# Block 2's first four units take the rows before layer norm, and the norm is applied to their results

## The chip, the cores and the metric

The kernel runs on one core of one Trainium2 chip. The metric is the device time of one execution in microseconds. TensorE (PE) does the matrix products and writes PSUM; VectorE (DVE), ScalarE (ACT) and GpSimd (POOL) do the elementwise work, and POOL has no access to PSUM; SyncE (SP) issues the DMAs. Each engine takes its instructions in the order in which they were written down for it, and waits for the other engines by semaphores.

## The reference

Three blocks run one after the other on a sequence of 512 positions with 2048 features, in float32. What matters here is the start of block 2, on the result of block 1:

```
def second_block(x, c, w_ada, b_ada, w_in, ...):
    mod = jax.nn.silu(c) @ w_ada[l] + b_ada[l]
    shift, scale, gate = jnp.split(mod[:, None, :], 3, axis=-1)
    h = _layernorm(x) * (1.0 + scale) + shift
    proj = h @ w_in[l]
    u, v, z_a, q, k, v_b, z_b = jnp.split(proj, IN_SPLITS, axis=-1)
    y_a = _spatial_gating(jax.nn.gelu(u), jax.nn.gelu(v), z_a, ...)
    ...
```

`x` there is the RMS-normed output of block 1. Layer norm needs mean and variance over all 2048 features of a position, so every one of them must be known before the first normed value is.

## The kernel before

Activations lie transposed: a tile has 128 features in its partitions and the 512 positions along the free dimension, so the 2048 features are 16 tiles (index `k`). A weight matrix is worked off in **units**: one unit makes 128 output features, as 16 steps of `k`. Float32 accuracy comes from splitting: weights and rows are each taken as `hi` (rounded to the matmul's format, on ACT) and `lo` (the rest, on DVE), and each step has three products 128x128 by 128x512 (`hi*hi`, `hi*lo`, `lo*hi`), so a unit has 48 of them. The weights' parts are called `wh` and `wl`; the chunks they come from, 4 steps of a unit each, are split on ACT and DVE while PE works.

Block 1 ends in its output projection, 16 units. `out1_tile` adds the input, centres it on a rough mean (`d`, kept in `ds`), and adds up the three sums that the norms need. `out1_end` handles the last tile: 24 sums over partitions on PE (`stat_sum`) in the last unit and 24 after it (`stat_last`), then seven operations on 128x4 columns and two powers on POOL give the factors `g` and `c` of the norm (`x*g + c`). PE spreads them over the partitions with 16 small products (`bcast_cols`). Meanwhile PE runs 27 products whose results nobody reads (`warm`). `make` then builds the normed row of step `k`: two DVE operations (times `g`, plus `c`, both read from PSUM), on ACT the scaling with `1 + scale` and `shift`, and the split into `hi` and `lo`.

`first_units` runs the first four units of block 2 (output tiles 8, 0, 16 and 9) side by side, step by step, as the rows become ready; the last four steps are done unit by unit. From the fifth unit on all 16 rows are there, and units run one after the other (`drive`), each request of a consumer (`sgu` for the spatial gating) in its turn. The results of the first four units stay in PSUM until `sgu` reads them.

The order on each engine is found by a scheduler at build time from the order of the program and its own durations; from `out1_end` up to the end of `first_units`' set-up it is held to the program's order for DVE, ACT and PE (`in_order`). Tiles come from pools with a fixed number of buffers for a tag: 7 for `e`, 9 for `w`, 20 for `y`, 5 each for `wh` and `wl`, 3 for raw weight chunks. A tile waits until its buffer is free.

Beside the units of blocks 1 and 2 a background queue (`bgq`, one step for each weight chunk) computes the modulations `mod2` and `mod3` (`mods`: 6 slices of 16 loads of 512 KB with one DVE operation 128x1024 each, and two steps on PE and DVE) and a bias table. `sc2` is `1 + scale` and `1 + gate` of block 2.

Of the kernel before, what the change touches and what calls it, by code (L numbers as in the profile page):

```python
# [34 lines left out]
FIRST2 = (8, 0, 16, 9)  # L35
# [5 lines left out]
class Kernel:  # L41
# [188 lines left out]
            except StopIteration as e:  # L230
                return e.value

    def first_units(self, w, cts, make, chunks, side=None, tail=None):

        rhs, pss, has = [], [], {}
        for _ in cts:
            self.n += 1
            pss.append(self.pm.tile([P, T], F32, name=f"pm{self.n}", tag="m"))  # L240

        def take(chunks):
            for u, k0, hl in chunks:
                has[u] = has.get(u, []) + [(k0, hl)]

        def product(k, u):
            k0, (hi, lo) = [c for c in has[u] if c[0] <= k][-1]
            c, ps = slice((k - k0) * P, (k - k0 + 1) * P), pss[u]
            self.mm(ps, hi[:, c], rhs[k][0], start=k == 0, stop=False)
# [415 lines left out]
    def mods(self, wada, c, b, mod):  # L665
# [6 lines left out]
        for sl in range(6):  # L672
# [10 lines left out]
            for half in range(2):  # L683
# [3 lines left out]
                self.tt(o, o, self.col(b, 8 * sl + 4 * half, 4), OP.add)  # L687
                yield


    def stat_begin(self, n):
        self.acc = [self.k(f"acc{i}") for i in range(n)]
# [36 lines left out]
    def out1(self, ys):  # L729
        ysp = [self.split(v) for v in ys]  # L730
        self.stat_begin(3)
        ds = []
        self.sc2 = self.cp.tile([P, 32], F32, name="sc2")
        for ct in range(KT - 1):
            self.out1_tile(ct, self.unit(self.A["wo1"], ct, ysp), ds)
        self.ts(self.sc2, self.mod2[:, 16:48], 1.0, None, OP.add)
        with self.in_order():
            args = self.out1_end(ysp, ds)
        return self.first_units(self.A["w2"], FIRST2, *args)

    def out1_tile(self, ct, ps, ds):
        nc = self.nc
# [17 lines left out]
        return (0, d), (2, sx), (1, sq)  # L760

    def out1_end(self, ysp, ds):
        nc = self.nc
        last, ps = self.last_unit(self.A["wo1"], ysp, self.stat_sum)
# [4 lines left out]
        m, v, a, g, c = (self.s(4) for _ in range(5))  # L769

        self.ts(a, ps[:, 8:12], LN_EPS / D, LN_EPS * EPS)
        self.ts(m, ps[:, 0:4], 1.0 / D)
        self.stt(v, ps[:, 4:8], 1.0 / D, a, OP.mult, OP.add)
        self.tt(c, m, m)
        self.tt(v, v, c, OP.subtract)
        nc.gpsimd.tensor_tensor(g, v, self.nhalf[:, :4], OP.pow)
        self.r1 = self.cp.tile([P, 4], F32, name="r1")
        self.ts(a, ps[:, 8:12], 1.0 / D, EPS)
        nc.gpsimd.tensor_tensor(self.r1, a, self.nhalf[:, :4], OP.pow)
        self.stt(c, m, -1.0, g, OP.mult, OP.mult)  # L780
        chunks = self.end(self.first_chunks(self.A["w2"], FIRST2, 0))
        gb, cb = self.bcast_cols(g), self.bcast_cols(c)
        self.warm(9, ysp[15][0])
        mod = self.mod2

        def make(k):
            t1 = self.t()
            self.tt(t1, ds[k], gb)
            self.tt(t1, t1, cb, OP.add)
            self.act(t1, t1, AF.Identity, scale=self.sc2[:, k:k + 1], bias=mod[:, k:k + 1])  # L790
            hi, lo = self.a(), self.a()
            self.act(hi, t1)
            yield
            yield
            self.tt(lo, t1, hi.bitcast(F32), OP.subtract)
            return hi, lo

        return make, chunks


    def sgu(self, g, h, w, ys):
# [879 lines left out]
def _wtile(w, perm=None):  # L1681

    K, N = w.shape
    return np.ascontiguousarray(
        w.reshape(K // 1024, 8, P, N // P, P).transpose(3, 0, 2, 1, 4).reshape(N // P, K // 1024, P, 1024))


def _rpb_rows(r):
# [92 lines left out]
```

## Time and profile before

| | us |
|---|---|
| median of 3 runs (lowest, highest) | 3410.37 (3408.67, 3417.95) |
| the profiled execution | 3414.3 |
| its span in the profile | 3412.6 |
| PE busy (mean granted clock 0.996) | 3370.2, 99% |
| PE weight loads | 2777.0, 81% |
| DVE busy | 2010.0, 59% |
| ACT busy | 1272.6, 37% |
| POOL busy | 131.5, 4% |
| DMA | 451.64 MB, 132 GB/s on average |

A row of the profile names a line of the kernel, an engine, an operation, and the tiles as output <- inputs without their numbers: `pm` are the sums of units in PSUM, `x` other PSUM tiles, `a` rows split for the matmul, `wr`, `wh`, `wl` raw weights and their two parts, `t` work tiles of the tags `w`, `e` and `y`, `s` small columns, `ga` and `gr` the background's sum and load. Times are in microseconds from the start of the span unless ns stands there. Matmuls are pipelined: one takes 0.39 us or so from start to end, and the next starts before.

### The profile page before, as it was taken

The numbers are of one execution on the slowest core, as the hardware profiler recorded it, in microseconds if no ns is written. First come the engines' busy times: TensorE is split into PE (matmuls) and PEld (weight loads), VectorE is DVE, ScalarE is ACT, GpSimd is POOL, SyncE is SP. The second block draws the span as 40 slices with busy tenths as digits, with TensorE's granted clock in tenths as the row PEclk, the third lists the DMA queues.
The fourth block names the chain that finished last, engine by engine and source line by source line (L and its number), as shares of the span: only waits on it lengthen the run. The fifth ranks groups of instructions, "written<-read, shape, count | busy, mean of one in ns | idle before, by whom it ended". The sixth has DMA issues, their size and how long they took to land.

```text
span 3412.6 us, 43830 instructions
## 1 busy us (share of the span) xinstructions
PE 3370.2 (99%) x16336; PEld 2777.0 (81%) x16336; DVE 2010.0 (59%) x3793; ACT 1272.6 (37%) x2459; POOL 131.5 (4%) x156
## 2 busy tenths in 40 slices
PE   9999999999999999999999999999999999999999
PEld 7877877877888888888888888887888888888887
DVE  8677566657777555643367667756755443344552
ACT  4222244444334223444442243333334444432331
POOL 0000000000000000101100000000000000000000
PEclk9999999999999999999999999999999999999999
DMA  6355345435663445532234333332222233324442
GB/s 223 124 179 173 132 153 185 152 120 191 211 218 128 161 156 175 170 119 96 84 105 146 99 107 109 96 98 84 85 72 87 96 108 104 128 99 143 141 146 92
DMA packets 166166, 451.64 MB, mean 132 GB/s; under 512 B 26496, under 2 KB 47296, under 8 KB 165952
## 3 DMA queue, kind: packets, MB, share of 16 engines
q1 hardware_dynamic: 165952, 448.84, 39.6%
q8 instruction: 128, 2.10, 0.3%
q14 instruction: 86, 0.70, 0.1%
HBM read 423.58 MB, written 25.18 MB: 132 GB/s over the span
## 4 chain that ended last, share of the span: by engine, by line
PE 86%; DVE 7%; DMA 3%; issue 2%; ACT 1%; POOL 0%; SPq 0%; DVEq 0%; ACTq 0%; POOLq 0%
PE pm L128 76%; PE x L128 8%; DMA gr<-in_wada_dram 3%; PE x L638 1%; DVE wl L117 1%; PE x L134 1%; DVE ga L120 1%; DVE t L117 1%; DVE fp L117 1%; DVE t L120 1%; DVE ft L1290 1%; ACT t L114 0%; ACT wh L114 0%; DMA t<-in_xt_dram 0%; DVE t L527 0%
## 5 line engine op out<-in xcount | busy, mean ns | idle before, releaser
L128 PE MATMUL pm<-a,wh 128*128 128x512 f32 x8512 | 2669.2, 394 | 6.2 <-ACT a L114 3.6
L128 PEld LDWEIGHTS pm<-a,wh 128*128 128x128 f32 x8512 | 1575.4, 189 | 335.9 <-issue 15.6
L128 PE MATMUL pm<-a,wl 128*128 128x512 f32 x4256 | 1665.5, 391 | 0.5 <-DVE wl L117 0.5
L114 ACT ACTIVATE wh<-wr 128x512 fp32r<-128x512 f32 (+2 forms) x1073 | 671.6, 627 | 1714.5 <-PE pm L128 1570.9
L117 DVE TENSOR_TENSOR wl<-wr,wh 128x512 fp32r<-128x512 f32 (+2 forms) x1073 | 738.1, 690 | 913.5 <-ACT wh L114 843.7
L128 PEld LDWEIGHTS pm<-a,wl 128*128 128x128 f32 x4256 | 801.3, 188 | 172.9 <-DVE wl L117 0.9
L120 DVE SCALAR_TENSOR_TENSOR ga<-gr,sc_c,ga 128x1024 f32<-128x1024 f32 x180 | 231.1, 1284 | 80.5 <-DMA gr<-in_wada_dram 79.7
L114 ACT ACTIVATE t<-t 128x512 f32<-128x512 f32 (+2 forms) x204 | 125.0, 613 | 147.7 <-DVE t L117 101.4
L114 ACT ACTIVATE t<-x 128x512 f32<-128x512 f32 (+4 forms) x301 | 143.7, 505 | 83.1 <-PE x L128 50.7
L117 DVE TENSOR_TENSOR t<-t,t 128x512 f32<-128x512 f32 (+2 forms) x233 | 155.8, 669 | 23.2 <-ACT t L114 19.0
L128 PE MATMUL x<-t,t 128*128 128x128 f32 (+8 forms) x1104 | 146.1, 295 | 7.5 <-DVE t L117 7.4
L128 PEld LDWEIGHTS x<-t,t 128*128 128x128 f32 (+3 forms) x1104 | 117.8, 175 | 33.7 <-issue 19.3
L114 ACT ACTIVATE t<-t,s 128x512 f32<-128x512 f32 (+2 forms) x192 | 98.5, 513 | 96.0 <-DVE s L527 63.0
L142 POOL TENSOR_TENSOR s<-s,nhalf 128x4 f32<-128x4 f32 (+1 forms) x51 | 61.2, 1201 | 1247.9 <-DVE s L125 1247.9
L638 PE MATMUL x<-cst,t 128*128 128x128 f32 x464 | 66.7, 275 | 5.8 <-DVE t L124 3.8
L120 DVE SCALAR_TENSOR_TENSOR t<-t,pm 128x512 f32<-128x512 f32 x64 | 43.7, 684 | 46.1 <-PE pm L128 46.0
L638 PEld LDWEIGHTS x<-cst,t 128*128 128x128 f32 x464 | 55.5, 144 | 17.1 <-DVE t L124 6.1
L114 ACT ACTIVATE t<-pm 128x512 f32<-128x512 f32 (+2 forms) x154 | 68.9, 482 | 0.2
L117 DVE TENSOR_TENSOR a<-t,a 128x512 fp32r<-128x512 f32 x96 | 63.7, 686 | 8.8 <-ACT a L114 8.7
L128 PE MATMUL x<-acc,t 128*128 128x256 f32 (+3 forms) x336 | 66.4, 297 | 0.0
L134 PE MATMUL x<-cst,t 128*128 128x128 f32 x400 | 60.3, 273 | 6.1 <-DVE t L117 2.9
L134 PEld LDWEIGHTS x<-cst,t 128*128 128x128 f32 x400 | 48.3, 140 | 19.8 <-DVE t L120 2.9
(232 smaller groups left out, 1663.9 us busy)
## 6 DMA issues: line engine op xcount, KB each, us to landing
wr<-in_w_dram SPq DMA_DIRECT2D x380, 512.0 KB, 3.3
gr<-in_wada_dram SPq DMA_DIRECT2D x192, 512.0 KB, 4.3
wr<-in_wo_dram SPq DMA_DIRECT2D x96, 512.0 KB, 3.4
t<-in_xt_dram SPq DMA_DIRECT2D x32, 256.0 KB, 4.0
res<-t SPq DMA_DIRECT2D x32, 256.0 KB, 2.1
t<-res SPq DMA_DIRECT2D x32, 256.0 KB, 2.7
gld<-t SPq DMA_DIRECT2D x32, 256.0 KB, 2.0
t<-gld SPq DMA_DIRECT2D x32, 256.0 KB, 2.8
```

Of the source, the lines that this page charges most:

```text
L114: return self.nc.scalar.activation(out, in_, fn, **kw)
L117: return self.nc.vector.tensor_tensor(out, a, b, op)
L120: return self.nc.vector.scalar_tensor_tensor(out, a, s, b, op0=op0, op1=op1)
L128: return self.nc.tensor.matmul(out, l, r, start=start, stop=stop, skip_group_check=True)
L134: self.nc.tensor.transpose(b[:, p * P:(p + 1) * P], src[:, p * P:(p + 1) * P], self.ident)
L142: self.nc.gpsimd.tensor_tensor(out, u, self.nhalf[:, :n], OP.pow)
L638: self.nc.tensor.transpose(b[:, j * P:(j + 1) * P], src, self.ident)
L1290: nc.vector.tensor_reduce(tv[:, :, i], pv, AX, OP.add, negate=True)
```

## The change

The first four units no longer wait for the norm. They multiply the weights with `ds[k]` times `1 + scale`, without `g` and `c`. Since the norm is the same for all features of a position, it can be applied to a unit's result: result times `g`, plus `c` times the sum of the scaled weights, plus the sum of the weights times `shift`. These two sums for each output feature (`uv2`) are computed in the background beside block 1 (`first_sums`, a new queue entry between `mods` of block 2 and of block 3, from a copy `w2f` of the four units' weights).

The 27 products of `warm` are gone, and so is the program's order by hand. The last sums are formed after step 1, the spreads after step 3, and each is copied by ACT to SBUF. The normed rows `h`, which the later units need, are built by `operand`, beside the first units: the multiplication on POOL, the addition on POOL for even `k` and on DVE for odd `k`, then scaling and split as before. `tail` applies the norm to each of the four results and leaves it in a `y` tile in SBUF. The raw rows' `hi` and `lo` use the tag `e`.

```diff
-    def first_units(self, w, cts, make, chunks, side=None, tail=None):
+    def first_units(self, w, cts, make, chunks, side=None, tail=None, step=None, pss=None):
...
                     for u in (1, 2, 3, 0):
                         product(k - 1, u)
+                    if step:
+                        step(k)
...
+    def first_sums(self, wf, cols, out):
...
+        for k in range(KT):
+            raw = self.gp.tile([P, 1024], F32, name=f"gf{self.n}_{k}", tag="gr", bufs=2)[:, 0:T]
+            nc.sync.dma_start(raw, wf[k])
+            for a, c in zip(acc, cols):
+                if k == 0:
+                    self.ts(a, raw, c[:, 0:1])
+                else:
+                    self.stt(a, raw, c[:, k:k + 1], a, OP.mult, OP.add)
+            yield
+        ps = self.x()
+        for i in range(n):
+            for u in range(4):
+                self.mm(ps[:, 4 * i + u:4 * i + u + 1], acc[i][:, u * P:(u + 1) * P], self.ones[:, 0:1])
+        nc.vector.tensor_copy(out, ps[:, 0:4 * n])
+        yield
...
-        self.warm(10, ysp[15][0])
         lasts = self.out1_tile(KT - 1, last, ds)
-        self.stat_last(ps, lasts)
-        self.warm(8, ysp[15][0])
...
         def make(k):
+            hi, lo = self.e(F32R), self.e(F32R)
+            sc = self.sc2[:, k:k + 1]
+            self.act(hi, ds[k], scale=sc)
+            yield
+            yield
+            self.stt(lo, ds[k], sc, hi.bitcast(F32), OP.mult, OP.subtract)
+            return hi, lo
...
+        def operand(k):
+            gb, cb = rows
             t1 = self.t()
-            self.tt(t1, ds[k], gb)
-            self.tt(t1, t1, cb, OP.add)
+            nc.gpsimd.tensor_tensor(t1, ds[k], gb, OP.mult)
+            (nc.vector if k % 2 else nc.gpsimd).tensor_tensor(t1, t1, cb, OP.add)
             self.act(t1, t1, AF.Identity, scale=self.sc2[:, k:k + 1], bias=mod[:, k:k + 1])
+            h.append(self.split(t1))
+
+        def step(k):
+            if k == 1:
+                self.stat_last(ps, lasts)
+                rows.extend(factors())
+            elif k == 3:
+                for i in range(2):
+                    b, r = self.bcast_cols(rows[i]), self.k(("acc0", "acc1")[i])
+                    self.act(r, b)
+                    rows[i] = r
+            elif k > 3:
+                operand(len(h))
+
+        def tail(u):
+            gb, cb = rows
+            q, o = self.t(), self.y()
+            self.act(q, cb, AF.Identity, scale=self.uv2[:, u:u + 1], bias=self.uv2[:, 4 + u:5 + u])
+            self.tt(o, pss[u], gb)
+            self.tt(o, o, q, OP.add)
+            z[FIRST2[u]] = o
+            for _ in range(2):
+                if len(h) < KT:
+                    operand(len(h))
...
         self.bgq.append(self.mods(self.A["wada2"], "c2", "b2", self.mod2))
+        self.uv2 = self.cp.tile([P, 8], F32, name="uv2")
+        self.bgq.append(self.first_sums(self.A["w2f"], self.cols2, self.uv2))
         self.bgq.append(self.mods(self.A["wada3"], "c3", "b3", self.mod3))
```

The order of the instructions shows what stands behind what. DVE before, from the last column operation of the norm on (`s` columns, `wl` the weights' `lo`, `x1382` and `x1383` the spread factors in PSUM, `t1389` and `t1392` rows 0 and 1):

```order
L120 SCALAR_TENSOR_TENSOR s1375_8703<-s1371_8699,s1374_8702 128x4
L117 TENSOR_TENSOR wl1377_8717<-wr1376_8714,wh1377_8716 128x128
L117 TENSOR_TENSOR wl1378_8721<-wr1376_8714,wh1378_8720 128x256
L117 TENSOR_TENSOR wl1379_8725<-wr1376_8714,wh1379_8724 128x384
L117 TENSOR_TENSOR wl1381_8730<-wr1380_8727,wh1381_8729 128x512
L117 TENSOR_TENSOR wl1396_8779<-wr1395_8776,wh1396_8778 128x512
L117 TENSOR_TENSOR t1389_8761<-t1194_7312,x1382_8736 128x512
L117 TENSOR_TENSOR t1392_8768<-t1205_7400,x1382_8736 128x512
```

No row there waits for POOL. DVE in the changed kernel, from the same column operation on (`t1402` and `t1409` are the raw rows' `lo` of steps 4 and 5; L833 is the addition to the normed rows 1, 3 and 5, `t1412`, `t1426`, `t1440`; `acc1` is the spread `c`; `wl1411` belongs to the weights of step 5):

```order
L120 SCALAR_TENSOR_TENSOR s1388_8748<-s1384_8744,s1387_8747 128x4
L117 TENSOR_TENSOR wl1396_8788<-wr1395_8785,wh1396_8787 128x512
L120 SCALAR_TENSOR_TENSOR t1402_8818<-t1240_7690,sc2_6425,t1401_8817 128x512
L117 TENSOR_TENSOR wl1404_8824<-wr1403_8821,wh1404_8823 128x512
L120 SCALAR_TENSOR_TENSOR t1409_8848<-t1251_7778,sc2_6425,t1408_8847 128x512
L833 TENSOR_TENSOR t1412_8870<-t1412_8870,acc1_1400_8815 128x512
L833 TENSOR_TENSOR t1426_8932<-t1426_8932,acc1_1400_8815 128x512
L833 TENSOR_TENSOR t1440_8992<-t1440_8992,acc1_1400_8815 128x512
L117 TENSOR_TENSOR wl1411_8855<-wr1410_8851,wh1411_8854 128x512
L117 TENSOR_TENSOR a1407_8844<-t1405_8839,a1406_8843 128x512
```

Three additions to normed rows now stand ahead of `wl1411`, and each needs its row's multiplication on POOL. POOL in the changed kernel, from the second power of the norm on (L832 multiplications with the spread `g`, `acc0`; L833 additions; before, only the two powers stood here):

```order
L822 TENSOR_TENSOR s1387_8747<-s1385_8745,nhalf_89 128x4
L832 TENSOR_TENSOR t1405_8839<-t1194_7324,acc0_1398_8808 128x512
L832 TENSOR_TENSOR t1412_8870<-t1205_7414,acc0_1398_8808 128x512
L832 TENSOR_TENSOR t1419_8901<-t1218_7514,acc0_1398_8808 128x512
L833 TENSOR_TENSOR t1405_8839<-t1405_8839,acc1_1400_8815 128x512
L833 TENSOR_TENSOR t1419_8901<-t1419_8901,acc1_1400_8815 128x512
L832 TENSOR_TENSOR t1426_8932<-t1229_7602,acc0_1398_8808 128x512
L832 TENSOR_TENSOR t1433_8962<-t1240_7690,acc0_1398_8808 128x512
L832 TENSOR_TENSOR t1440_8992<-t1251_7778,acc0_1398_8808 128x512
```

The multiplication for row 5, `t1440`, is POOL's eighth operation on whole tiles; 16 more follow it. PE in the changed kernel at the end of the four units (`pm1374` to `pm1377` are their sums, `t1470` and `t1471` the `hi` and `lo` of step 15, `pm1522` the fifth unit, `t1506` the first Gelu's result, turned by L134):

```order
L128 MATMUL pm1374_8703<-t1471_9105,wh1460_9066 128x512
L128 MATMUL pm1374_8703<-t1470_9104,wl1460_9067 128x512
L128 MATMUL pm1375_8704<-t1471_9105,wh1467_9096 128x512
L128 MATMUL pm1375_8704<-t1470_9104,wl1467_9097 128x512
L128 MATMUL pm1376_8705<-t1471_9105,wh1481_9156 128x512
L128 MATMUL pm1376_8705<-t1470_9104,wl1481_9157 128x512
...
L128 MATMUL pm1377_8706<-t1471_9105,wh1491_9195 128x512
L128 MATMUL pm1377_8706<-t1470_9104,wl1491_9196 128x512
L128 MATMUL pm1522_9307<-a1406_8843,wh1524_9310 128x512
L128 MATMUL pm1522_9307<-a1407_8844,wh1524_9310 128x512
L134 MATMUL x1509_9257<-cst_84,t1506_9249 128x128 x4
```

All four sums are finished by the `lo` of step 15 within a dozen products, and the fifth unit and the turning of the first Gelu's result follow at once; before, the four sums were finished one after the other, 12 products apart.

More of the change, by code (lines that the diff above doesn't have):

```diff
@@ L231, in end @@
                 return e.value
-    def first_units(self, w, cts, make, chunks, side=None, tail=None):
-        rhs, pss, has = [], [], {}
+    def first_units(self, w, cts, make, chunks, side=None, tail=None, step=None, pss=None):
+        rhs, has = [], {}
+        pss = [] if pss is None else pss
         for _ in cts:
@@ L688, in mods @@
                 yield
+    def first_sums(self, wf, cols, out):
+        nc = self.nc
+        cols = cols()
+        n = len(cols)
+        self.n += 1
+        acc = [self.gp.tile([P, 1024], F32, name=f"fa{self.n}", tag="ga", bufs=1)]
+        acc = [acc[0][:, 0:T], acc[0][:, T:]]
+        if n > 2:
+            acc.append(self.gp.tile([P, 1024], F32, name=f"fb{self.n}", tag="gr", bufs=2)[:, 0:T])
+        for k in range(KT):
[13 more added lines that the diff above has]
+        yield
     def stat_begin(self, n):
@@ L732, in out1, with cols2 @@
         ds = []
-        self.sc2 = self.cp.tile([P, 32], F32, name="sc2")
         for ct in range(KT - 1):
             self.out1_tile(ct, self.unit(self.A["wo1"], ct, ysp), ds)
+        return self.out1_end(ysp, ds)
+    def cols2(self):
+        self.sc2 = self.cp.tile([P, 32], F32, name="sc2")
         self.ts(self.sc2, self.mod2[:, 16:48], 1.0, None, OP.add)
-        with self.in_order():
-            args = self.out1_end(ysp, ds)
-        return self.first_units(self.A["w2"], FIRST2, *args)
+        return self.sc2[:, 0:16], self.mod2[:, 0:16]
     def out1_tile(self, ct, ps, ds):
@@ L763, in out1_end, with late @@
         nc = self.nc
-        last, ps = self.last_unit(self.A["wo1"], ysp, self.stat_sum)
-        self.warm(10, ysp[15][0])
+        w, mod = self.A["w2"], self.mod2
+        def late():
+            return self.stat_sum(), self.end(self.first_chunks(w, FIRST2, 0))
+        last, (ps, chunks) = self.last_unit(self.A["wo1"], ysp, late)
         lasts = self.out1_tile(KT - 1, last, ds)
-        self.stat_last(ps, lasts)
-        self.warm(8, ysp[15][0])
-        m, v, a, g, c = (self.s(4) for _ in range(5))
@@ L771, in out1_end @@
[L771 to L784, printed above, removed]
-        def make(k):
-            t1 = self.t()
-            self.tt(t1, ds[k], gb)
-            self.tt(t1, t1, cb, OP.add)
-            self.act(t1, t1, AF.Identity, scale=self.sc2[:, k:k + 1], bias=mod[:, k:k + 1])
-            hi, lo = self.a(), self.a()
-            self.act(hi, t1)
+        h, z, rows = [], {}, []
@@ L793, in make, with factors @@
+        def make(k):
+            hi, lo = self.e(F32R), self.e(F32R)
+            sc = self.sc2[:, k:k + 1]
+            self.act(hi, ds[k], scale=sc)
             yield
             yield
-            self.tt(lo, t1, hi.bitcast(F32), OP.subtract)
+            self.stt(lo, ds[k], sc, hi.bitcast(F32), OP.mult, OP.subtract)
             return hi, lo
-        return make, chunks
+        def factors():
+            m, v, a, g, c = (self.s(4) for _ in range(5))
+            self.ts(a, ps[:, 8:12], LN_EPS / D, LN_EPS * EPS)
+            self.ts(m, ps[:, 0:4], 1.0 / D)
+            self.stt(v, ps[:, 4:8], 1.0 / D, a, OP.mult, OP.add)
+            self.tt(c, m, m)
+            self.tt(v, v, c, OP.subtract)
+            nc.gpsimd.tensor_tensor(g, v, self.nhalf[:, :4], OP.pow)
+            self.r1 = self.cp.tile([P, 4], F32, name="r1")
+            self.ts(a, ps[:, 8:12], 1.0 / D, EPS)
+            nc.gpsimd.tensor_tensor(self.r1, a, self.nhalf[:, :4], OP.pow)
+            self.stt(c, m, -1.0, g, OP.mult, OP.mult)
+            return g, c
@@ new lines, in operand @@
+        def operand(k):
+            gb, cb = rows
+            t1 = self.t()
+            nc.gpsimd.tensor_tensor(t1, ds[k], gb, OP.mult)
+            (nc.vector if k % 2 else nc.gpsimd).tensor_tensor(t1, t1, cb, OP.add)
+            self.act(t1, t1, AF.Identity, scale=self.sc2[:, k:k + 1], bias=mod[:, k:k + 1])
+            h.append(self.split(t1))
[10 more added lines that the diff above has]
+                operand(len(h))
@@ new lines, in tail @@
+        def tail(u):
[8 more added lines that the diff above has]
+                    operand(len(h))
+        pss = []
+        self.first_units(w, FIRST2, make, chunks, tail=tail, step=step, pss=pss)
+        while len(h) < KT:
+            operand(len(h))
@@ L801, in sgu @@
+        return h, z
     def sgu(self, g, h, w, ys):
@@ L1685, in _wtile, with _firsts @@
         w.reshape(K // 1024, 8, P, N // P, P).transpose(3, 0, 2, 1, 4).reshape(N // P, K // 1024, P, 1024))
+def _firsts(w, cts):
+    return np.ascontiguousarray(w.reshape(KT, P, -1, P)[:, :, list(cts)].reshape(KT, P, len(cts) * P))
 def _rpb_rows(r):
@@ L1734, in prepare @@
     A["w2"], A["wo2"] = _wtile(a["w_in_2"][0]), _wtile(a["w_out_2"][0])
+    A["w2f"] = _firsts(a["w_in_2"][0], FIRST2)
     A["sgu_b"] = np.ascontiguousarray(a["sgu_norm_b_2"][0].reshape(8, P))
```

## The prediction

> **What bounds the kernel now.** I read the page's totals first, then its chain, then windows and the timeline around the place that the diff touches.
>
> ```profile
> span 3412.6 us, 43830 instructions
> ...
> PE 3370.2 (99%) x16336; PEld 2777.0 (81%) x16336; DVE 2010.0 (59%) x3793; ACT 1272.6 (37%) x2459; POOL 131.5 (4%) x156
> ...
> PE 86%; DVE 7%; DMA 3%; issue 2%; ACT 1%; POOL 0%; SPq 0%; DVEq 0%; ACTq 0%; POOLq 0%
> ```
>
> TensorE sets the end: it is busy 99% of the span, and 86% of the chain lies on it. A change outside PE counts only where PE waits, or does work that nobody needs. The passage from block 1 to block 2 is such a place. Three pieces of the chain hold it (columns: start, length, what):
>
> ```profile
> 989.82 40.80 PE pm L128 x180
> ...
> 1037.65 4.87 PE x L128 x34
> ...
> 1050.68 45.42 PE pm L128 x192
> 1096.10 0.44 PE x L134 x4
> ```
>
> The first row gives PE's rate in a dense stretch: 40.80/180 = 0.2267 us a matmul. The last product of block 1's projection ends at 1037.65, which I call S. The first product of block 2 starts at 1050.68, so 13.03 us hold no main product. The 192 products of the first four units then take 45.42 us, where 192 x 0.2267 = 43.5; 1.9 us are lost. The four units end 58.45 us behind S. What PE runs in the hole:
>
> ```profile
> 1037.49 2.45 PE L128 MATMUL x<-a 128*128 128x512 f32 x10
> 1039.78 2.73 PE L128 MATMUL x<-ones,t 128*128 128x1 f32 x24
> 1042.37 2.11 PE L128 MATMUL x<-a 128*128 128x512 f32 x8
> 1044.41 2.05 PE L128 MATMUL x<-cst,s 128*128 128x128 f32 x16
> 1046.22 2.31 PE L128 MATMUL x<-a 128*128 128x512 f32 x9
> ```
>
> Only the 24 sums (2.73) and the 16 spreads of the two factors (2.05) are needed; the 27 `x<-a` are the filler. The 1.9 us are a clock effect:
>
> ```profile
> 1045.00:1050.00 5.00, 3.53 (x23) 2.80 (x21) 5.00 (x10) 1.41 (x2) 0.33 (x1) 1.00 0.47 157
> 1050.00:1055.00 5.00, 4.32 (x12) 3.45 (x13) 4.61 (x9) 4.38 (x8) 0.00 (x0) 0.66 0.01 3
> ```
>
> PE is busy 3.53 and 4.32 of 5 us, 2.15 us idle in all, and its granted clock (third figure from the right) then falls to 0.66.
>
> **The best case.** The un-normed product needs only `ds` and `sc2`; the order shows its first four `hi` long before S. So PE goes straight on: 13.03 - 2.73 - 2.05 = 8.25 us go, and the 1.9 with them if PE never idles: **-10.15**.
>
> **The sums beside block 1.** Sixteen background steps of 256 KB and two 128x512 DVE operations each move ahead of `mods` for block 3, whose steps look like this:
>
> ```profile
> L120 DVE SCALAR_TENSOR_TENSOR ga<-gr,sc_c,ga 128x1024 f32<-128x1024 f32 x180 | 231.1, 1284 | 80.5 <-DMA gr<-in_wada_dram 79.7
> L120 DVE SCALAR_TENSOR_TENSOR a<-t,par,a 128x512 fp32r<-128x512 f32 x16 | 11.9, 745 | 1.5 <-ACT a L114 1.5
> 880.00:1037.00 157.00, 157.00 (x705) 130.21 (x705) 115.98 (x161) 48.45 (x79) 0.00 (x0) 0.99 0.71 236
> ```
>
> A step becomes 2 x 0.745 = 1.49 instead of 1.28 us, with half the bytes; DVE is busy 116 of 157 us beside a full PE, so this hides. If the cover were gone it would be 16 x 0.2 = 3 us. What does not hide are the 8 sums over partitions on PE, 16 instructions at 2.73/24: **+1.8**.
>
> **The new queue: POOL before DVE before PE.** The normed rows `h` are still made, beside the first units: 16 multiplications and 8 additions on POOL, 8 additions on DVE. Durations in the stretch of the four units, then over the whole run:
>
> ```profile
> L117 DVE TENSOR_TENSOR a<-t,a 128x512 fp32r<-128x512 f32 x16 | 10.6, 684 | 0.2 <-ACT a L114 0.2
> L117 DVE TENSOR_TENSOR wl<-wr,wh 128x512 fp32r<-128x512 f32 x15 | 10.3, 691 | 5.6 <-ACT wh L114 4.1 <-PE pm L128 1.3
> L114 ACT ACTIVATE t<-t,mod,sc 128x512 f32<-128x512 f32 x14 | 11.2, 808 | 3.9 <-DVE t L117 3.9
> L114 ACT ACTIVATE wh<-wr 128x512 fp32r<-128x512 f32 x16 | 10.0, 628 | 7.4 <-PE pm L128 6.6 <-DVE wl L117 0.7
> L114 ACT ACTIVATE a<-t 128x512 fp32r<-128x512 f32 x16 | 9.8, 625 | 0.3
> L114 ACT ACTIVATE a<-t,par 128x512 fp32r<-128x512 f32 x16 | 11.4, 712 | 4.1 <-DMA t<-in_xt_dram 4.1
> L457 POOL TENSOR_TENSOR t<-t,t 128x512 f32<-128x512 f32 x8 | 10.7, 1332 | 171.5 <-DVE t L117 141.3 <-DVE s L125 20.1 <-ACT wh L114 10.1
> ```
>
> PE reaches the spreads at S + 3 x 12 x 0.2267 + 2.73 = S+10.9; one spread (1.0) and its copy on ACT (0.6), with the hand-overs, let POOL start at S+12.7. The order puts DVE's addition to operand 5 behind POOL's eighth operation and ahead of `wl` for chunk 5. DVE is strictly in order, so that `wl` waits: eight operations at 1.07 (the shortest kind, row below; DVE does little meanwhile) give S+21.2, the addition and the split 1.4, POOL's delays by three additions 0.6: S+23.2. PE needs it at S + 62 x 0.2267 + 4.78 = S+18.8. **+4.4**; with 1.06 to 1.52 for each POOL operation 3.7 to 7.5.
>
> **DVE and POOL together.** From there 39 DVE rows follow up to the last `lo`, some 0.61 us from start to start (684 and 691 overlap a little), 23.8 us; PE's 130 products left take 29.5, so alone DVE keeps up. But 16 POOL operations run beside it, and both read SBUF:
>
> ```profile
> 218.36 1.07 POOL L457 TENSOR_TENSOR t<-t,t 128x512 f32<-128x512 f32 x1 [40.78 <-DVE t L117]
> 218.80 1.17 DVE L117 TENSOR_TENSOR wl<-wr,wh 128x512 fp32r<-128x512 f32 x1
> 323.02 1.38 POOL L457 TENSOR_TENSOR t<-t,t 128x512 f32<-128x512 f32 x1 [39.89 <-DVE t L117]
> 323.39 1.55 DVE L120 SCALAR_TENSOR_TENSOR t<-t,t 128x512 f32<-128x512 f32 x1
> 1484.99 4.67 POOL L875 TENSOR_TENSOR t<-cst,t 128x256 f32<-128x256 f32 x6 [47.62 <-DMA t<-in_rpb_dram]
> 1487.62 0.74 DVE L117 TENSOR_TENSOR wl<-wr,wh 128x512 fp32r<-128x512 f32 x1 [2.37 <-ACT wh L114]
> ```
>
> Beside a 128x512 POOL operation a DVE one took 1.17 and 1.55 instead of 0.69: 0.48 to 0.86 more. Inside a train of six POOL operations of half that size it took 0.74, next to nothing more. I take 0.6, near the nearer size: 16 x 0.6 = 9.6, DVE 33.4, and the last `lo` at S+56.6. Twelve products (2.7) follow it, so the four units end near S+59.3 where PE alone, from S+23.2, would end at S+52.7 plus 0.2 for that `lo`: **+6.4**; bounds 0 (POOL costs nothing) to 0.86 each, +10.6. The Trainium skill, page "SBUF — State Buffer", section "SBUF: two separate sides", says that GpSimd and a DVE operation with two SBUF inputs share a port pair and lock each other out for a whole instruction. The first two pairs agree with it in kind and none in full size; in full size the term would be 13.9 and the sum +15.2.
>
> On POOL the powers for block 2's first two gating norms now stand behind all 24 operations. These end near S + 21.2 + 16 x 1.4 = S+44; PE wants the first norm in the middle of unit 1, after S+60. Hidden.
>
> **The end of the four units.** The last 4 x 8 `hi`/`lo` tiles want 8 buffers of tag `e`, which has 7. So the last `lo` waits for one of the last products, and all four units end within 12 products. Before, the first of them ended early:
>
> ```profile
> 1088.19 1.28 ACT L114 ACT_TABLE_LOAD   x1
> 1089.48 0.60 ACT L114 ACTIVATE t<-pm 128x512 f32<-128x512 f32 x1
> ```
>
> There the table load and the first Gelu lay 6 us ahead of 1096.10. Now 11 DVE rows (two `tt` a unit, three splits of `h`) stand between the last `lo` and the fourth unit's result, 6.8 us, then a Gelu of 0.6, while PE has 12 products, 4 of unit 1 and a transposition, 4.1 us: **+3.3**. ACT has, from S+12 to the end of the units, 16 scalings and 4 `q` by 0.81, 16 copies and 11 weight splits by 0.63 and nine raw `hi` by 0.71, 39.6 of 47 us. It keeps up with little to spare; if it is late at the end, the term is 6.8.
>
> **The clock again.** A stall of 4 us is longer than the 2.15 us idle time that cost 1.9 above, so this comes back: **+1.9**, up to 3.7 with a second one.
>
> **The sum:** -10.15 + 1.8 + 4.4 + 6.4 + 3.3 + 1.9 = **+7.7 us**. The profiled execution took 3414.3 us (span 3412.6), which gives 3422.0; against the median 3410.37 of the runs, 3418. All lower ends together: -10.15 + 1.8 + 3.7 + 0 + 3.3 + 0 = -1.4, so 3409; all upper ends: -10.15 + 1.8 + 7.5 + 10.6 + 6.8 + 3.7 = +20.3, so 3431.
>
> **Rivals.**
> *Full cover.* POOL runs ahead, DVE never waits, the tail hides: -10.15 + 1.8 = -8.3, 3402. For it: POOL is 4% busy over the run. Against it: the order of the DVE queue, which does not depend on durations. 5%.
> *POOL beside DVE is free.* The pair at 1487.62 says so. The wait behind the eighth POOL operation and the tail stay: 3409 to 3411. 18%.
> *Convoy, slower than before.* Each POOL operation stops DVE for its whole 1.07 us: 16 x 1.07 = 17.1 instead of 9.6, so +7.5, and 3425; with ACT late in the tail (+3.5) 3429. It decides from about 0.75 us per POOL operation, where the sum passes the bound of 0.3%. For it: 1.55 at 323.39, against it 1.17 at 218.80. 17%. (This is the lock of the Trainium skill's SBUF page in full size.)
> *The change does not do what it says:* main products do not start at S because `wl` for chunk 0 comes late. The hole then keeps some microseconds: 3421. 3%.
>
> **How the numbers follow.** The forecast (57%) spreads from 3411 to 3425. A measurement of this kernel tells about 0.3%, 10.2 us, from no change, so the lines are 3400.1 and 3420.6. A third of the forecast lies above the upper one (0.19), the convoy nearly all (0.16), and half of the last rival (0.02): slower 0.37. Faster needs the full cover and more: 0.03. The rest, 0.60, is no change that can be told. From 3407 to 3430 some 2 in 10 are left out.
>
> **What would show it.** Right: main products from about S on with no `x<-a`; a PE idle time of about 4 us in chunk 5 of the first units, released by DVE `wl`, with DVE waiting for POOL; POOL operations of 1.3 us and more and DVE splits over 1 us behind it; all four units ending within 3 us; PE waiting for a Gelu after them. The four units would end at S+59 or so. Wrong: POOL at 1.07 with DVE at 0.69 side by side; or the end of the units at S+50, by which the kernel would gain.

## The result and the profile after

The changed kernel takes 3429.97 us (median of 5 executions, 3429.24 to 3439.13) against 3412.41 us of the kernel before in the same comparison: ratio 1.0058, 95% interval 1.0041 to 1.0074. It is slower by 14 to 25 us. The profiled execution took 3429.27 us, 15.0 more than that of before. One of four executions of e2, below, took 16512.44 us at a granted clock of 0.19 and one of before's 4052.9 us at 0.77; they are left out of every figure. The page's totals:

```profile
span 3427.5 us, 43943 instructions
...
PE 3370.6 (98%) x16325; PEld 2776.5 (81%) x16325; DVE 2047.4 (60%) x3826; ACT 1286.1 (38%) x2481; POOL 172.1 (5%) x180
```

PE is as busy as before to 0.4 us in a span that is 14.9 us longer. The 27 filler products (6.9 us) are gone; that the figure stays is due mostly to PE at half its clock. The loss is idle time and half clock. PE's timeline of the changed kernel around the passage (start, length, what, in brackets the idle time before and who ended it):

```profile
1037.30 0.63 PE L128 MATMUL pm<-a,wl 128*128 128x512 f32 x1
1037.73 0.79 PE L128 MATMUL pm<-t,wh 128*128 128x512 f32 x2
...
1057.49 0.73 PE L128 MATMUL pm<-t,wh 128*128 128x512 f32 x2 [1.26 <-ACT wh L114]
1064.92 0.79 PE L128 MATMUL pm<-t,wl 128*128 128x512 f32 x1 [6.70 <-DVE wl L117]
...
1069.99 0.50 PE L128 MATMUL pm<-t,wh 128*128 128x512 f32 x1 [0.48 <-DVE t L120]
...
1077.93 0.79 PE L128 MATMUL pm<-t,wh 128*128 128x512 f32 x1 [4.93 <-DVE t L120]
...
1095.21 0.50 PE L128 MATMUL pm<-t,wl 128*128 128x512 f32 x1 [1.04 <-DVE wl L117]
...
1106.08 0.39 PE L128 MATMUL pm<-t,wl 128*128 128x512 f32 x1
...
1108.35 0.66 PE L134 MATMUL x<-cst,t 128*128 128x128 f32 x4 [1.43 <-ACT t L114]
1109.91 1.22 PE L128 MATMUL pm<-a,wh 128*128 128x512 f32 x2 [0.90 <-ACT wh L114]
```

The hole of before is gone: the first product of block 2 (1037.73) follows the last of block 1's projection, so S is 1037.93 here. But PE then idles 14.41 us inside the four units (the first five waits above) and 2.33 us behind them, and the units end at 1106.3, S+68.4, where before took 58.45 us. What DVE and POOL did around the longest stall, from the timeline by engine:

```profile
1057.25 4.19 POOL L832 TENSOR_TENSOR t<-t,acc 128x512 f32<-128x512 f32 x3
1061.39 1.26 POOL L833 TENSOR_TENSOR t<-t,acc 128x512 f32<-128x512 f32 x1
1062.61 3.39 POOL L832 TENSOR_TENSOR t<-t,acc 128x512 f32<-128x512 f32 x2
```

```profile
1061.47 1.74 DVE L833 TENSOR_TENSOR t<-t,acc 128x512 f32<-128x512 f32 x1 [1.16 <-POOL t L832]
1063.12 1.75 DVE L117 TENSOR_TENSOR wl<-wr,wh 128x512 fp32r<-128x512 f32 x1
1064.79 1.75 DVE L117 TENSOR_TENSOR a<-t,a 128x512 fp32r<-128x512 f32 x1
```

DVE stood still for POOL's eighth operation, did the addition to operand 5, and only then `wl` of chunk 5, for which PE waits. And a DVE row that meets a POOL operation takes 1.75 us, where before it took 0.69. The windows of five microseconds (sum, busy time of PE, PEld, DVE, ACT and POOL, granted clock, DMA share, GB/s) show what follows the stalls:

```profile
1060.00:1065.00 5.00, 0.08 (x1) 0.08 (x1) 3.84 (x4) 1.65 (x3) 5.00 (x4) 0.70 0.01 2
1065.00:1070.00 5.00, 4.52 (x12) 3.26 (x12) 5.00 (x4) 3.19 (x5) 4.92 (x4) 0.62 0.32 85
...
1075.00:1080.00 5.00, 2.07 (x5) 1.68 (x6) 5.00 (x6) 0.60 (x1) 2.42 (x3) 0.56 0.17 52
...
1110.00:1115.00 5.00, 5.00 (x18) 3.90 (x19) 4.12 (x17) 1.67 (x3) 1.02 (x1) 0.68 0.26 82
```

Behind the stalls of 6.70 and 4.93 us, and behind the two waits at the end, PE runs some microseconds at half its clock: the ten products from 1064.92 took 4.19 us instead of 10 x 0.2267 = 2.27.

Executions differ by several microseconds ahead of this place, so the kernels below are also compared by one stretch of their profiles, called **the passage**: from the first statistics products to the first of the eight-fold transpositions near 1364 us. In the timeline of before these are

```profile
1030.46 2.73 PE L128 MATMUL x<-ones,acc 128*128 128x1 f32 x24
...
1364.51 1.03 PE L638 MATMUL x<-cst,t 128*128 128x128 f32 x8
```

| kernel | start | mark | passage | ratio of times (95%) |
|---|---|---|---|---|
| before | 1030.46 | 1364.51 | 334.05 | |
| before again (n0) | 1031.06 | 1363.85 | 332.79 | 0.9998 (0.9989 to 1.0007) |
| changed | 1030.88 | 1379.53 | 348.65 | 1.0058 (1.0041 to 1.0074) |
| e1: operand work on DVE | 1030.81 | 1369.25 | 338.44 | 1.0017 (1.0008 to 1.0026) |
| e2: all additions on POOL | 1036.63 | 1390.88 | 354.25 | 1.0055 (1.0037 to 1.0074) |
| e3: no operand work | 1036.82 | 1370.18 | 333.36 | 1.0004 (0.9994 to 1.0015) |
| e4: the sums alone | 1032.38 | 1366.86 | 334.48 | 1.0019 (1.0010 to 1.0028) |
| e5: rows read from PSUM | 1035.98 | 1373.05 | 337.07 | 1.0022 (1.0013 to 1.0032) |
| e6: e5 and an early Gelu | 1031.55 | 1368.27 | 336.72 | 1.0027 (1.0018 to 1.0036) |
| e7: e1 and POOL aside | 1039.65 | 1395.28 | 355.63 | 1.0073 (1.0058 to 1.0087) |
| n1: the tile alone | 1028.38 | 1362.47 | 334.09 | 1.0006 (0.9996 to 1.0017) |
| n2: the input alone | 1026.34 | 1360.41 | 334.07 | 0.9996 (0.9986 to 1.0005) |
| n4: the sums alone again | 1028.61 | 1361.85 | 333.24 | 1.0010 (1.0001 to 1.0018) |

The passage of the unchanged kernel differs by 1.3 us from one profile to another. A stretch at half clock explains most of it: in before it falls on the first main products of block 2 (clock 0.66 from 1050 to 1055), in n0 on the filler and the spreads (0.87 and 0.79 from 1040 to 1050, then 1.00). The changed kernel loses 14.6 us in the passage.

### The profile page after: what moved, and what is told of

Read it like the earlier page. It is cut to its first block, busy times and chain, and to the rows that moved or that the text cites. A ratio compares the mean times of both kernels' runs of the same rounds, so it can differ in the third digit from the quotient of the medians.

```text
span 3427.5 us, 43943 instructions
## 1 busy us (share of the span) xinstructions
PE 3370.6 (98%) x16325; PEld 2776.5 (81%) x16325; DVE 2047.4 (60%) x3826; ACT 1286.1 (38%) x2481; POOL 172.1 (5%) x180
## 4 chain that ended last, share of the span: by engine, by line
PE 62%; DVE 4%; issue 1%; ACT 1%; DMA 0%; POOL 0%; SPq 0%; DVEq 0%; ACTq 0%; POOLq 0%
PE pm L128 54%; PE x L128 5%; PE x L641 1%; DVE fp L117 1%; PE x L134 1%; DVE wl L117 1%; DVE ft L1356 1%; DVE t L117 1%; DVE t L120 1%; ACT t L114 0%; DMA gr<-in_wada_dram 0%; ACT wh L114 0%; POOL s L142 0%; DVE ga L120 0%; ACT a L114 0%
## 5 line engine op out<-in xcount | busy, mean ns | idle before, releaser
L128 PE MATMUL pm<-a,wh 128*128 128x512 f32 x8384 | 2627.0, 394 | 4.3 <-ACT wh L114 2.4
L128 PEld LDWEIGHTS pm<-a,wh 128*128 128x128 f32 x8384 | 1550.1, 188 | 328.0 <-issue 16.2
L128 PE MATMUL pm<-a,wl 128*128 128x512 f32 x4192 | 1639.2, 391 | 0.5 <-DVE wl L117 0.5
L128 PEld LDWEIGHTS pm<-a,wl 128*128 128x128 f32 x4192 | 788.4, 188 | 170.4 <-DVE wl L117 0.9
L117 DVE TENSOR_TENSOR a<-t,a 128x512 fp32r<-128x512 f32 x96 | 69.1, 739 | 10.2 <-ACT a L114 10.1
L134 PE MATMUL x<-cst,t 128*128 128x128 f32 x400 | 60.7, 275 | 9.6 <-DVE t L117 5.0
L134 PEld LDWEIGHTS x<-cst,t 128*128 128x128 f32 x400 | 48.5, 140 | 23.9 <-DVE t L117 4.7
```

The costliest lines, as they stand in the source:

```text
L117: return self.nc.vector.tensor_tensor(out, a, b, op)
L128: return self.nc.tensor.matmul(out, l, r, start=start, stop=stop, skip_group_check=True)
L134: self.nc.tensor.transpose(b[:, p * P:(p + 1) * P], src[:, p * P:(p + 1) * P], self.ident)
```

## The experiments

Two theories: **A**, a POOL operation and a DVE operation that both use SBUF exclude each other for a whole operation, so that POOL takes its time out of DVE's; **B**, the in-order queues and the numbers of buffers set the pace, and the slow rows are a side effect.

**p1: the price of the pair by itself.** Behind the end of the kernel before stand stages of six operations each, 128x512 on DVE (two SBUF inputs, one PSUM input, a single input) and on POOL (128x512 or 128x256), alone and together:

```diff
+            for pf, df in ((None, "two"), (None, "stt"), (None, "one"), (None, "psum"),
+                           ("two", None), ("half", None), ("rows", None),
+                           ("two", "two"), ("two", "stt"), ("two", "one"), ("two", "psum"),
+                           ("half", "two"), ("rows", "two"), ("rows", "psum")):
...
+                for i in range(6):
+                    if pf:
+                        pool[pf](po, d)
+                    if df:
+                        dve[df](do, d)
```

> The kernel before with 14 stages of small operations behind its end, six each, first DVE and POOL alone, then both together; the time is 70 to 110 us longer and is of no interest, the durations of the rows are. Theory A: beside a 128x512 POOL tensor_tensor, DVE operations with two SBUF inputs take 1.7 us (0.65 plus POOL's 1.05) and POOL's 1.7; those with one input from PSUM, or with a single input, stay at 0.65. Half-size POOL operations delay DVE by their own length, 0.55 each. Rival (memory traffic is shared smoothly): all DVE forms grow alike, to 1.0 to 1.3 us.

DVE's timeline; lines 1644, 1646 and 1647 are two SBUF inputs, a single one, and one from PSUM. The first three rows are DVE alone, the next three beside 128x512 POOL operations, the last beside half-size ones:

```profile
3408.42 4.32 DVE L1644 TENSOR_TENSOR t<-t,t 128x512 f32<-128x512 f32 x6
...
3419.67 3.68 DVE L1646 TENSOR_SCALAR t<-t 128x512 f32<-128x512 f32 x6
...
3424.24 4.32 DVE L1647 TENSOR_TENSOR t<-x,t 128x512 f32<-128x512 f32 x6
...
3452.55 9.97 DVE L1644 TENSOR_TENSOR t<-t,t 128x512 f32<-128x512 f32 x6
...
3476.26 8.37 DVE L1646 TENSOR_SCALAR t<-t 128x512 f32<-128x512 f32 x6
...
3486.50 4.32 DVE L1647 TENSOR_TENSOR t<-x,t 128x512 f32<-128x512 f32 x6
...
3496.40 7.28 DVE L1644 TENSOR_TENSOR t<-t,t 128x512 f32<-128x512 f32 x6
```

POOL's timeline of the same kernel, alone, beside two SBUF inputs and beside a PSUM input:

```profile
3430.56 7.96 POOL L1650 TENSOR_TENSOR t<-t,t 128x512 f32<-128x512 f32 x6
...
3453.71 9.93 POOL L1650 TENSOR_TENSOR t<-t,t 128x512 f32<-128x512 f32 x6
...
3487.67 7.97 POOL L1650 TENSOR_TENSOR t<-t,t 128x512 f32<-128x512 f32 x6
```

Six DVE operations grow from 4.32 to 9.97 us, 0.94 each, and six POOL operations from 7.96 to 9.93: both engines come to one pair per 1.66 us, in turn. That is less than the two alone (0.72 and 1.33): what excludes DVE is some 1.0 us of POOL's 1.33, not all of it. With one input from PSUM neither loses anything (4.32, 7.97). The single-input form was expected to be free and is not (3.68 to 8.37). A half-size POOL operation costs DVE 0.49, and the masked form of which the prediction's train at 1484.99 consisted costs the same (six DVE rows in 7.26). So A holds for the pair. Smooth sharing of the memory is out: the single-input form and the PSUM form each read one tile from SBUF and write one, and only the first is slowed.

**e7: POOL aside.** The kernel of e1 (next), and 16 multiplications on POOL into a tile that nobody reads. No engine waits for their results:

```diff
             h.append(self.split(t1))
+            nc.gpsimd.tensor_tensor(rows2[0], ds[k], gb, OP.mult)
```

> The kernel with the operand work on DVE (e1), and 16 multiplications on POOL into a tile that nobody reads: nothing waits for POOL, no order changes. Theory A (lock): the 16 POOL operations run back to back from S+12.7 for 16 x 1.65 = 26 us, the DVE rows beside them take 1.66 and not 0.68, DVE loses about 16 x 0.94 = 15 us in the first half of the four units, PE idles there, and the passage is 11 to 16 us longer than in e1: 3425 to 3432. Rival B (queues and buffers, not the lock): as e1, 3415 to 3419.

POOL's timeline, then DVE's:

```profile
1060.95 27.05 POOL L836 TENSOR_TENSOR acc<-t,acc 128x512 f32<-128x512 f32 x16 [6.16 <-ACT acc L114]
```

```profile
1073.31 1.75 DVE L117 TENSOR_TENSOR wl<-wr,wh 128x512 fp32r<-128x512 f32 x1
1074.98 1.76 DVE L117 TENSOR_TENSOR a<-t,a 128x512 fp32r<-128x512 f32 x1
...
1088.47 0.74 DVE L120 SCALAR_TENSOR_TENSOR t<-t,sc,t 128x512 fp32r<-128x512 f32 x1
1089.13 0.68 DVE L117 TENSOR_TENSOR a<-t,a 128x512 fp32r<-128x512 f32 x1
```

While POOL runs, DVE takes 1.75 us a row, 1.67 from one start to the next; from 1088, when it has ended, 0.68, or 0.61 from start to start. The difference is 1.06 a row. The passage is 355.63 - 338.44 = 17.2 us longer than in e1, or 1.07 for each of the 16 operations. A had said 11 to 16 us, with the 0.94 of p1. The time of 3435.83 us is that of e1, 3417.64, and 17.2 more, and 1 us; it lies above A's range for this reason and because e1 itself is slower than I had put it. B's 3415 to 3419 is out. A POOL operation of this size costs DVE 1.07 us whether or not anybody waits for it.

**e1: the operand work on DVE.** The same 24 operations, none of them on POOL:

```diff
-            nc.gpsimd.tensor_tensor(t1, ds[k], gb, OP.mult)
-            (nc.vector if k % 2 else nc.gpsimd).tensor_tensor(t1, t1, cb, OP.add)
+            nc.vector.tensor_tensor(t1, ds[k], gb, OP.mult)
+            nc.vector.tensor_tensor(t1, t1, cb, OP.add)
```

> The eight-step operand work is unchanged, but its 16 multiplications and 8 POOL additions run on DVE; POOL does nothing in the stretch. Theory A (a 128x512 POOL operation and a two-input DVE operation exclude each other whole; that made the DVE rows 1.7 us): every 128x512 DVE row of the stretch takes 0.68 to 0.76 us; 55 rows from the first operand row to the last lo at 0.61 each put that lo near S+47 and the end of the four units near S+50, against S+66.7 in the changed kernel; the time falls to 3407 to 3412, 3 to 7 us below the kernel before. Rival B (the lock is a side effect, the in-order queues and the nine w buffers set the pace): 24 more rows on DVE cost 24 x 0.61 = 15 us more, the kernel is slower than the changed one, 3440.

3417.64 us, ratio 1.0017. B is out: the kernel is 0.4% faster than the changed one. A's mechanism is right (every row at 0.68 to 0.76) and its time too good. The passage is 10.2 us shorter than in the changed kernel; 24 POOL operations taken away at 1.07 and 24 DVE rows added at 0.61 give 11.0. PE's waits in this kernel (who waited for whom, us in total, times, longest):

```profile
PE pm L128 <- DVE wl L117: 3.3, 2, 1.7
PE pm L128 <- ACT wh L114: 2.5, 1, 2.5
PE x L134 <- ACT t L114: 1.5, 2, 0.9
```

All of it stands behind the four units' main part, from 1088 on. The chain leaves the units at 1085.9, S+48, but their last product waits 1.57 us for its `wl` and ends at 1090.5, S+52, where I had S+50. But DVE is full, or nearly, from 1055 to 1100; the windows behind the units:

```profile
1085.00:1090.00 5.00, 3.43 (x16) 2.48 (x15) 5.00 (x10) 4.74 (x8) 0.00 (x0) 1.00 0.01 4
1090.00:1095.00 5.00, 1.57 (x6) 1.01 (x7) 4.86 (x9) 4.33 (x8) 0.00 (x0) 0.69 0.54 170
1095.00:1100.00 5.00, 2.73 (x9) 1.72 (x9) 5.00 (x14) 4.20 (x8) 0.00 (x0) 0.50 0.06 14
```

Here the remaining operands, the four results and the next weights share DVE, and PE has 1.57 and 2.73 us of work in 5, then the half clock. The hole has moved from ahead of the four units to behind them.

**e3: no operand work.** Leaves out the multiplication and the addition of the rows gb and cb, so that h is the scaled and split raw row:

```diff
-            nc.gpsimd.tensor_tensor(t1, ds[k], gb, OP.mult)
-            (nc.vector if k % 2 else nc.gpsimd).tensor_tensor(t1, t1, cb, OP.add)
-            self.act(t1, t1, AF.Identity, scale=self.sc2[:, k:k + 1], bias=mod[:, k:k + 1])
+            self.act(t1, ds[k], AF.Identity, scale=self.sc2[:, k:k + 1], bias=mod[:, k:k + 1])
```

> Leaves out the multiplication by the gb row and the addition of the cb row (h is made from the un-normed rows by the scaling and the split alone). The new passage without POOL: DVE has 0.61 x (16 lo + 14 wl + 16 subtractions), 28 us beside 43.5 us of PE. Theory A and my sum: -10.15 + 0.3 (sums) + 2 to 3 (tail), 3406 to 3408 against 3414 of the profile before; the units end at S+47 or S+48 and PE idles only in the tail. If the new passage is slow by itself (the un-normed products, the late lo, e buffers), the units still end past S+52 and the time stays above 3411.

3413.57 us, ratio 1.0004: a miss. PE does run through the units without a wait, which is the 8 us that the change is about, but they come back behind them. The windows inside the units, and the chain behind them:

```profile
1050.00:1055.00 5.00, 5.00 (x16) 3.95 (x15) 2.52 (x7) 2.62 (x5) 1.98 (x2) 0.66 0.13 42
...
1060.00:1065.00 5.00, 5.00 (x23) 4.13 (x23) 3.69 (x6) 5.00 (x9) 0.00 (x0) 1.00 0.24 71
1065.00:1070.00 5.00, 5.00 (x23) 4.13 (x22) 3.94 (x7) 5.00 (x10) 0.00 (x0) 1.00 0.24 88
```

```profile
1088.57 7.27 DMA wr<-in_w_dram
...
1095.95 1.15 ACT wh L114 x2
1097.11 1.28 ACT L114
1098.41 0.64 ACT t L114
...
1099.09 1.12 PE x L134 x4
```

The units end at 1093.8, S+49.8, where I had S+47 or S+48: the first window has a stretch at half clock (0.66) although PE is never idle, which costs 1.7 us. With DVE at 3.7 to 3.9 of 5 us, ACT is now full. And the next weights are asked for only at 1088.57, behind six loads of small tables in SP's queue; ACT splits them, loads its table and makes the Gelu for which PE has waited 4.65 us. The passage is 333.36, within the scatter of before.

**e2: all additions on POOL.** No operand addition stands in DVE's queue:

```diff
-            (nc.vector if k % 2 else nc.gpsimd).tensor_tensor(t1, t1, cb, OP.add)
+            nc.gpsimd.tensor_tensor(t1, t1, cb, OP.add)
```

> All 16 additions on POOL: no operand addition stands in DVE's queue, POOL has 32 operations. If the first stall (8 us) came from DVE's addition waiting behind POOL, it shrinks to 2 or 3 us and the time falls to about 3422. Theory A with the in-order queue: the subtractions of the h split still stand in DVE's queue behind POOL's results (two POOL operations of 1.0 to 1.7 us each per operand), so the stalls move but stay; 13 operands x 2 x 1.7 = 44 us lie ahead of the last lo, which comes at S+57 to S+62, and the time is 3425 to 3435.

3434.41 us (three executions), ratio 1.0055, no different in time from the changed kernel, and inside the 3425 to 3435. The passage is 354.25, 5.6 us longer than in the changed kernel; eight operations moved from DVE (0.61) to POOL (1.07) give 3.7. Another 1.7 us are a stretch at half clock while PE is never idle (0.69 from 1050 to 1055), which the changed kernel doesn't have there. PE's waits:

```profile
PE pm L128 <- DVE wl L117: 8.7, 4, 2.9
PE pm L128 <- DVE t L120: 4.8, 5, 2.0
...
```

The one stall of 6.70 is cut into four of at most 2.9, and the total stays: 17.5 us with the waits for ACT, against 16.7 in the changed kernel. The addition at the head of DVE's queue decides where the wait falls, not how long PE waits in all.

**e5 and e6: rows from PSUM, and an early Gelu.** The lock spares a DVE operation with a PSUM input. In e5 the rows gb and cb stay in PSUM, DVE multiplies and adds from there, and POOL takes the 16 subtractions of the split; e6 also has one small Gelu ahead of the units, which loads the table early:

```diff
-            nc.gpsimd.tensor_tensor(t1, ds[k], gb, OP.mult)
-            (nc.vector if k % 2 else nc.gpsimd).tensor_tensor(t1, t1, cb, OP.add)
+            self.tt(t1, gb, ds[k])
+            self.tt(t1, cb, t1, OP.add)
...
-            h.append(self.split(t1))
+            hi, lo = self.a(), self.a()
+            self.act(hi, t1)
+            nc.gpsimd.tensor_tensor(lo, t1, hi.bitcast(F32), OP.subtract)
+            h.append((hi, lo))
...
```

> The operand's multiplication and addition on DVE with the rows gb and cb read from PSUM, where they were made; POOL does the 16 subtractions of the h split. Theory A with the probe (a DVE operation with one PSUM input isn't locked): DVE has 74 rows in place of 90, 32 of them free of the lock; 74 x 0.61 = 45 us plus at most half of the 16 x 0.94 for the pairs that still meet, 45 to 53 us against 55 in e1. The passage is 2 to 10 us shorter than in e1: 3407 to 3415. If PSUM inputs lock as well, the 16 POOL operations cost 15 us more than they save (16 x 0.61 = 10): 3422 and more.

> As e5, with one Gelu of a 128x1 column ahead of the units, so that the table is loaded while ACT has idle time. If the table load of 1.28 us in the tail is on the path, 1 to 1.5 us less than e5; if the tail waits for DVE or for weights, no difference.

3417.94 and 3417.68 us, ratios 1.0022 and 1.0027; the passages, 337.07 and 336.72, are 1.4 and 1.7 us shorter than in e1, below the 2 to 10 expected, and the times don't differ from e1's. Even this little can't be put down to them: e1 has a stretch at half clock with PE never idle (0.75 from 1045 to 1050, 1.7 us in all with the window before) where e5 and e6 have 1.00. In e6, POOL's row and two of DVE's rows beside it:

```profile
1066.21 2.88 POOL L837 TENSOR_TENSOR a<-t,a 128x512 fp32r<-128x512 f32 x2 [3.87 <-PE pm L128]
```

```profile
1066.59 1.87 DVE L117 TENSOR_TENSOR t<-x,t 128x512 f32<-128x512 f32 x3
1068.39 1.85 DVE L117 TENSOR_TENSOR wl<-wr,wh 128x512 fp32r<-128x512 f32 x2
```

The three rows with a PSUM input take 0.62 each beside POOL, `wl` 0.93. So the escape works inside the kernel too, and still gains nothing that can be told: with fewer rows on DVE the chain goes on through the four results and their Gelus at the end of DVE's queue. The early table load brought 0.35 us in the passage, less than two profiles of one kernel differ by; the tail waits for DVE.

**e4 and n4: the sums alone, and n0 to n2 against scatter.** e4 and n4 are one kernel: before, with `first_sums`, its tile and its input, and the addition that makes `sc2` moved ahead of them; nothing else of the change. n0 is before itself, n1 before with only the tile `uv2`, n2 with only the unread input:

```diff
+        self.uv2 = self.cp.tile([P, 8], F32, name="uv2")
+        self.bgq.append(self.first_sums(self.A["w2f"], self.cols2, self.uv2))
...
```

> The kernel before with nothing of the change but the sums of the weights beside block 1. My term: the 16 loads and 32 DVE operations hide, the 16 PE instructions do not: +1.8 us, ratio 1.0005. If they hide too (in the changed kernel the passage begins only 0.3 us later): 0 to 0.3 us, ratio 1.0000 to 1.0001. Rival (the sums delay block 1 or push later background work into busy stages): 3 us and more, ratio above 1.0009.

> The kernel before with the sums alone a second time: 1.0019 again (1.001 to 1.0028) if the sums, or what comes with them, cost some 6 us; 1.0002 (the 0.8 us that the trace shows from 722 us on) if the first result was the scatter of executions.

> The kernel before, unchanged, against itself: ratio 1.0000, within 0.0007. Its profile shows how far one execution differs from another ahead of 722 us, where the kernels with the sums arrived 0 to 9 us later than the one profile of before.

> The kernel before with only the small tile of the sums (128x8) allocated and set to zero: every later SBUF tile moves by 32 bytes. If the 6.4 us of the sums alone come from where the tiles lie: 3415 to 3417, ratio 1.0015 or more. If they come from the work of the sums: ratio 1.0000.

> The kernel before with only the 4 MB of extra weights declared as an input that nothing reads: the inputs lie elsewhere in DRAM. If the 6.4 us come from where the inputs lie: ratio 1.0015 or more; if not: 1.0000.

The sums cost 1.0019 (1.0010 to 1.0028) in the first comparison and 1.0010 (1.0001 to 1.0018) in the second, 3 to 6 us, the rival's price and not my 1.8. n0 and n2 are level; n1 is 1.0006 (0.9996 to 1.0017), which doesn't settle whether the place of the tiles has a part in it. The traces hold less. From a transposition near 722 us to the start of the passage, the four profiles without the sums (before, n0, n1, n2) take 307.3 to 308.2 us and the nine with them 308.4 to 309.5, about 1.1 more; in the 386 to 390 us behind the passage (to the first 128x3 product near 1753 us) the background work that the sums push back costs another 1.2 on average, within a scatter of 3. Ahead of 722 us the kernels run the same instructions, and their arrival there scatters from 718.8 to 731.3. So 2.3 us are in the traces, and 1 to 4 us of the timed cost stay open.

## Why the prediction was wrong

I forecast +7.7 us and no change that can be told; measured are +15 in the profile and 1.0058 in time. The places where time would be lost were right, and the sizes of several terms were not. Against the sum, in the changed kernel's profile:

- **The best case, -10.15.** Right here: products from S on with no filler, and full clock from 1040 to 1060. But 1.9 of it rested on "if PE never idles", and that doesn't assure it: e1, e2 and e3 lost 1.7 us to half clock in this stretch with PE busy all the time.
- **The sums, +1.8.** 0.3 in this pair of profiles, 2.3 on average of the traces, 3 to 6 timed. This is the only term whose cause isn't fully shown.
- **DVE behind POOL, +4.4.** Right place, chunk 5, and POOL started at S+12.6. Measured 1.26 + 6.70 = 8.0, beyond the upper end of 7.5. The eight POOL operations took 10.9 us, 1.36 each where I had 1.07; most of that is POOL itself, which takes 1.33 in a train alone (p1). The addition and `wl` behind them took 1.7 each, the full price of a pair, where I had 1.4 for both. The 1.26 came over ACT, whose `wh` of this chunk stood behind scalings that waited for the additions.
- **DVE and POOL together, +6.4.** The idle time of the later stalls is 0.48 + 4.93 + 1.04 = 6.45. That the number agrees is chance: part of the lock's cost already stands in the first stall.
- **The end, +3.3.** 1.43 + 0.90 = 2.3 of waits. All four units did end together, and PE did wait for a Gelu. But it was late on ACT, behind three weight splits and the table load, where the sum had counted DVE's rows.
- **The clock, +1.9.** 6.2: 1.9, 2.2 and some 2.1 behind three stalls, where I had allowed for two at most (3.7).

With some 1.6 us of small delays, where PE starts again behind these waits and between products, the terms give -10.15 + 0.3 + 8.0 + 6.45 + 2.3 + 6.2 + 1.6 = 14.7, and the mark came 15.0 later.

**The steps that failed.** Two terms carry the miss: the clock, 4.3 us too small, and the wait behind POOL, 3.6 too small. The clock's step is "+1.9, up to 3.7 with a second one". The sum itself held three waits of more than 3 us (4.4, 6.4 and 3.3), each longer than the 2.15 us of idle time that the 1.9 was read from, and charged the clock for one of them.

The wait behind POOL has two steps. One is POOL's operation at 1.07 us, the shortest row, where eight in a train took 1.36 each; that is about half of the 3.6. The other half is the price of a DVE and a POOL operation that meet, "I take 0.6, near the nearer size", which I had not charged to the two rows there at all; the runs show 1.07. The same price stands in the next term, where chance hid it. I took it from two single rows, 0.48 and 0.86 more, read against POOL's whole length. But in the first the DVE row began 0.44 us after the POOL operation of 1.07 us, of which 0.63 were left, and in the second 0.37 after one of 1.38, of which 1.01 were left. Against what was left, the rows waited out 0.48 of 0.63 and 0.81 of 1.01 (the second is a SCALAR_TENSOR_TENSOR, which takes 0.745 by itself and not 0.69). They spoke for the lock nearly in full. The row of 0.74 in a POOL train was one row; p1 has 1.21 for each of six beside operations of that size and form. Why that one row lost so little isn't shown.

So the rival that I called the convoy had the price right. That its +15.2 in the sum meets the 15.0 measured is luck: it put 13.9 on DVE and POOL together and 1.9 on the clock, where 6.45 and 6.2 were measured. The Trainium skill, "SBUF — State Buffer", section "SBUF: two separate sides", states that lock for a whole instruction. e7 (1.07 each) and p1 (0.94) agree in kind; in size they show less than the 1.33 us that a POOL operation takes alone. The page also states that within the engines only the shared port pair causes contention, and the PSUM form of p1, which lost nothing, fits that.

What I overlooked beyond the price: the engine beside POOL was full already. In the four units of before DVE was busy 4.6 to 5.0 of 5 us from 1050 to 1085 but for one window (3.49), and only in the last ten microseconds 1.5 to 2.4. The change adds 24 rows (16 `lo` and 8 for the results) and moves 24 to POOL. On POOL an operation takes 1.07 us of DVE's time, on DVE itself 0.61. The passages of e1, e2 and e7 follow from these two numbers to within 2 us, and e3 shows that ACT, the loads and the clock behind the units take most of the 8 us even when that work is left out. No version that I ran is faster than the kernel before.

## What to carry to other kernels

Before elementwise work is moved to POOL to relieve DVE, count it as DVE time: a 128x512 operation cost DVE 1.07 us here, more than the 0.61 it takes on DVE; of the forms that I tried only DVE operations with an input in PSUM escaped. When a hole of the bounding engine is closed, look at how full the other engines are in the stretch behind it: if they were its near bound, the hole comes back at the end, and each new stall can bring a stretch of half clock with it, so a sum with three stalls has to price three. And price a contention from a train of pairs, or take a single row against what was left of the other operation when it began.

## What the hardware showed beyond this

A DVE operation with a single SBUF input was stopped too (six in 8.37 us instead of 3.68, 0.78 each, against 0.94 with two inputs). A POOL operation that took 1.33 us in a train alone (7.96 for six) held DVE for only 0.94 to 1.07 of it. PE at half clock took 4.19 us for ten products behind an idle time of 6.70, and fell to it as well behind waits of 1.43 and 0.90 with 0.66 us of work between them (two products in 1.22 us).

PE also fell to half clock without being idle at all. In each of the 13 profiles of the passage the clock falls to half for 3.4 us, 2.4 to 4.0 us behind the start of its first 24 one-column products, with PE never idle there but for 0.34 us in n4 (changed kernel: busy 5.00 of 5 us from 1035 to 1040, clock 0.69). Behind the second 24 the same happens in e1, e2, e3, e7, n0 and n4, and not in the changed kernel, e5 and e6 (1.00 there); in before, e4, n1 and n2 half clock comes instead behind the 2.15 us of idle time that the prediction read it from. One such stretch costs a busy PE 1.7 us. What decides where it falls isn't shown, so 1.7 us between two single profiles say nothing until their clocks have been compared.
